# Half-array fp32 products of a two-block layer, recorded as units

## The chip, the cores and the metric

The kernel runs on one core of a Trainium2 chip. The metric is the device time of one execution in microseconds, the median of the runs. The program is one launch: it reads 159 MB of fp32 weights and constants and writes a 256 x 1024 result.

## What is computed

The input is 256 tokens of 1024 features. Two transformer-like blocks follow one another.

```
block 1: u = rmsnorm(x);  p = u @ w_in + b_in
         y_attn = sliding-window attention, 16 heads of 64, 2 key/value heads, with sinks
         y_hgrn = gated recurrence, 8 heads of 128 x 128, in chunks of 64 tokens
         x += (sigmoid(ga) * (y_attn @ wa) + sigmoid(gb) * (y_hgrn @ wh)) @ w_out
         x += (silu(u2 @ wg) * (u2 @ wu)) @ wd          (u2 = rmsnorm(x))
block 2: mod = silu(c) @ w_ada + b_ada                  (shifts, scales, gates)
         y_ssd = state-space mixer, 8 heads of 64, state 128
         y_att = chunk attention, 8 heads of 64, with a relative bias
         x += g_m * ([y_ssd, y_att] @ w_out2)
         x += g_f * conv_ffn(...)
```

Everything is fp32. The large products with weights are computed as three products of a high and a low part (`fp32r`): the weights are split on the chip as they arrive.

## The kernel before, in words

Features lie on the 128 partitions and the 256 tokens along the free dimension. A weight tile of 128 x 1024 is loaded (`raw`), rounded to `wh` on ScalarE (now and then on VectorE), and the remainder `wl` is formed on VectorE. Eight feature blocks with three matmuls each (`group`, line 292) then make one output block: these are the projections, called the gemm here. They are by far most of TensorE's instructions.

Between them stand small products in plain fp32, each of which TensorE executes as two matmul records. Several use only half of the 128 x 128 array:

- attention scores (`attn_pair`): two heads at a time; the 64 features of head 0 lie on rows 0 to 63, those of head 1 on rows 64 to 127. A head has two products, one of 256 and one of 128 columns (names `kd,aq` in block 1, `qk` in block 2). They occupy 64 rows and 128 columns of the array.
- attention values (`attn_pair`): the output of a head has 64 features, so the products occupy 128 rows and 64 columns of the array, the left half for one head, the right half for the other (names `apt,vtok` and `apt,v`), again with 256 and with 128 columns of the moving operand.
- rows of the state-space mixer (`ssd`): for each of four pairs of heads, six products of 128 rows by 64 columns with 128 moving columns (names `m_all,X` and `ce_all,prev`).
- the second half of the recurrence scores (`hgrn_pair`): for each pair of heads four products with an output of 64 partitions and 64 moving columns (names `Q_all,hD`), all on the same half, beside four products on the whole array (names `hD,hE`).

The order is not written by hand. The program is recorded as operations on symbolic tiles; `schedule` then places them with a list scheduler: for each engine it takes the operation with the lowest key among those that can start. The keys follow the running sum of recorded TensorE time, and inside a `Chain` (attention `a1` and `a2`, recurrence `h`, state space `s`) each recorded operation has a key a fixed step after the one before it: 0.401 for `a1`, 0.613 for `h`, 0.521 for `s`, 0.419 for `a2`, in microseconds. The scheduler prices an fp32 product at 1.6667 ns a column and nothing else. `mm` records one product as one operation, so the scheduler may put projections, transposes or other products between two half-array products. Each engine is given its instructions in the order so made.

Of the kernel before, what the change touches and what calls it, by code (L numbers as in the profile page):

```python
# [16 lines left out]
P = 128  # L17
# [27 lines left out]
for _n, _w in ROW:  # L45
# [2 lines left out]
NR = _o  # L48
NCST = 128 + 128 + 384 + 128

# The program is first recorded (operations on symbolic tiles), then put in an order by a list
# scheduler, and then emitted in that order.

# weights of the list scheduler (microseconds; la and altw in nanoseconds)
OPT = dict(
    split=216.82, altp1=0, altw1=250.0, o_n3=-12.83, s_n3=0.097, o_f=-0.19, s_f=0.007, lead=9.18, tp=2.16,
    la=85.0, ahead=1.87, law=0.52, altp=2.98, altw=676.0, ada=-6.56, o_h=3.27, s_h=0.613, o_a1=-4.74,
# [9 lines left out]
SET6 = "natural_log_exp_and_others"  # L67


# products of the first blocks after a norm: the last features come last  # L70
PARTS = [list(range(6)), [6, 7]]


# [68 lines left out]
class Program:  # L142
# [5 lines left out]
        self.tags = {}  # L148
        self.seqs = defaultdict(int)

    # tiles
    def tile(self, shape, dtype, tag, name, bufs=1, pool="sb"):
        t = VTile(name, list(shape), dtype, pool, tag, bufs)
        assert self.tags.setdefault((pool, tag), bufs) == bufs, (tag, bufs)
# [2 lines left out]
        ids = np.arange(int(np.prod(shape[1:])), dtype=np.int32).reshape([1] + list(shape[1:]))  # L157
        return Ref(t, (), 0, shape[0], ids)

    # operations  # L160
    def op(self, eng, dur, fn, reads, writes, table=None, key=None, nbytes=0):
        o = Op()
        o.i, o.eng, o.dur, o.fn, o.table, o.nbytes = len(self.ops), eng, dur, fn, table, nbytes
# [53 lines left out]
        return self.op("ACT", dur, fn, reads, writes, TABLE.get(func), key)  # L217

    def either(self, out, in_, scale=None, bias=None, func=AF.Copy, key=None):
        # out = scale * in + bias on ScalarE or on VectorE  # L220
        o = self.act(out, in_, func, bias=bias, scale=scale, key=key)
        nap = sum(isinstance(x, Ref) for x in (bias, scale))
        dur = out.n * (1.0417 if in_.t.psum else 0.5208) + 68 + 61 * nap

        def f():
            v = self.nc.vector
            if scale is None and bias is None:
                v.tensor_copy(out.real(), in_.real())
            elif bias is None:
                v.tensor_scalar(out=out.real(), in0=in_.real(), scalar1=_real(scale), scalar2=None, op0=ALU.mult)  # L230
            elif scale is None:
                v.tensor_scalar(out=out.real(), in0=in_.real(), scalar1=_real(bias), scalar2=None, op0=ALU.add)
            else:
                v.tensor_scalar(out=out.real(), in0=in_.real(), scalar1=_real(scale), scalar2=_real(bias), op0=ALU.mult, op1=ALU.add)

        o.alts["DVE"] = (dur, f, None)
        return o
# [49 lines left out]
    def group(self, calls, key=None):  # L287
# [7 lines left out]
        o.cnt = len(calls)  # L295
        return o

    def tr(self, out, in_, ident, key=None):
        f = lambda: self.nc.tensor.transpose(out.real(), in_.real(), ident.real())  # L299
        return self.op("PE", 107, f, [in_, ident], [out], key=key)  # L300
# [4 lines left out]
        f = lambda: self.nc.sync.dma_start(out=_real(out), in_=_real(src))  # L305
        return self.op("SP", 475, f, reads, writes, key=self.T if key is None else key, nbytes=nbytes)

    # order
    def schedule(self):
        ops = self.ops  # L310
        for o in ops:
# [25 lines left out]
        la, tp, law, altp, altw = OPT["la"], OPT["tp"], OPT["law"], OPT["altp"], OPT["altw"]  # L337
# [1 line left out]
        slot_free = {k: [0.0] * b for k, b in self.tags.items()}  # L339

        def gate(o):
            # earliest time at which the tiles of o can be had; None when a tag is used up
            g = 0.0
            need = None
            for t in o.tiles:
                if not t.live:
                    k = (t.pool, t.tag)
                    if t.bufs == 1 and t.seq != nxt[k]:
                        return None
                    need = need or defaultdict(int)  # L350
                    need[k] += 1
            if need:
                for k, n in need.items():
                    sf = slot_free[k]
                    if len(sf) < n:
                        return None
                    g = max(g, sorted(sf)[n - 1])
            return g
# [109 lines left out]
def record(pr, d):  # L468
# [29 lines left out]
    def memset(t, val):  # L498
        pr.op("POOL", 300, lambda: nc.gpsimd.memset(t.real(), val), [], [t], key=-1.0)

    # parameters and constants
    cst_t = pr.tile([P, NCST], F32, "cst", "cst_t")
    vec_t = pr.tile([P, NV], F32, "vec", "vec_t")
    row_t = pr.tile([P, NR0], F32, "row", "row_t")
# [36 lines left out]
        o, w = ROFF[name]  # L541
        return row_t[:, o:o + w]

    # building blocks
    def wload(src, n):
        T = pr.T
        raw = pr.tile([P, RAW], F32, "raw", "raw", NRAW)
# [119 lines left out]
            self.i += 1  # L667
            return self.base + self.sp * self.i

    # attention of two heads  # L670
    def attn_pair(q, krows, vcols, bias, init, sink, yh, yl):
        xs = [t2([P, 384], "ax") for _ in range(2)]
        st = pr.tile([P, 2, 8], F32, "ast", "ast", 3)
        pss = [bank() for _ in range(2)]
        rows = [slice(64 * e, 64 * e + 64) for e in range(2)]
        for e in range(2):
            mm(pss[e][:, 0:256], q[rows[e], 128:256], krows(e)[rows[e], 0:256], True, True)
        for e in range(2):
            mm(pss[e][:, 256:384], q[rows[e], 0:128], krows(e)[rows[e], 0:128], True, True)
        for e in range(2):  # L680
            x, ps, b = xs[e], pss[e], bias(e)
            for i, (lo, hi) in enumerate(((0, 256), (256, 384))):
                def f(x=x, ps=ps, lo=lo, hi=hi, b=b, i=i, e=e):
                    nc.vector.tensor_tensor_reduce(
                        out=x[:, lo:hi].real(), in0=ps[:, lo:hi].real(), in1=b[i].real(), op0=ALU.add, op1=ALU.min,
                        scale=-1.0, scalar=_real(init(e)), accum_out=st[:, e, i:i + 1].real())

                rd = [ps[:, lo:hi], b[i]] + ([init(e)] if isinstance(init(e), Ref) else [])
                vec((hi - lo) * 1.0417 + 137, f, rd, [x[:, lo:hi], st[:, e, i:i + 1]]).cnt = 2
            for i, (lo, hi) in enumerate(((0, 256), (256, 384))):  # L690
                act(x[:, lo:hi], x[:, lo:hi], AF.Exp, bias=st[:, e, i:i + 1], scale=-1.0, accum_out=st[:, e, 2 + i:3 + i])
        if sink is not None:
            tt(st[:, :, 4:6], st[:, :, 0:2], sink.to_broadcast([P, 2, 2]), ALU.add)
            act(st[:, :, 4:6], st[:, :, 4:6], AF.Exp)
            tt(st[:, :, 2:4], st[:, :, 2:4], st[:, :, 4:6], ALU.add)
        vec(94, lambda: nc.vector.reciprocal(out=st[:, :, 6:8].real(), in_=st[:, :, 2:4].real()), [st[:, :, 2:4]], [st[:, :, 6:8]])
        pts = []
        for e in range(2):
            x = xs[e]
            either(x[:, 0:256], x[:, 0:256], st[:, e, 6:7])  # L700
            either(x[:, 256:384], x[:, 256:384], st[:, e, 7:8])
            ps = bank()
            tr(ps[:, 0:128], x[:, 256:384], ident)
            tr(ps[:, 128:256], x[:, 0:128], ident)
            tr(ps[:, 256:384], x[:, 128:256], ident)
            pt = t2([P, 384], "apt")
            either(pt, ps[:, 0:384])
            pts.append(pt)
        y = bank()
        for e in range(2):  # L710
            mm(y[rows[e], 0:256], vcols(e, 0), pts[e][:, 0:256], True, False)
        for e in range(2):
            mm(y[rows[e], 128:256], vcols(e, 1), pts[e][:, 256:384], False, True)
        either(yh, y[:, :S])
        tt(yl, y[:, :S], yh.bitcast(F32), ALU.subtract)

# [1 line left out]
    h = big("h", "h")  # L718
    dma(vec_t[:, 0:8], d["vec"][:, 0:8], 8 * 512, key=-100)
    warm = bank()  # L720
# [56 lines left out]
    v_evac(2, pv)  # L777
    hl = hl_of(u)

    # gates and queries of the recurrence  # L780
    A_all = big("yhh", "A_all", shape=[P, 4, 2, S])
    K_all = big("yhl", "K_all", shape=[P, 4, 2, S])
    Q_all = big("ml", "Q_all", shape=[P, 4, 2, S])
# [37 lines left out]
    def hgrn_pair(p):  # L821
# [25 lines left out]
            f = 2 * p + j  # L847
            stt(D4[:, j, 0:192], K[:, j, 0:192], omlb[:, f:f + 1], D4[:, j, 0:192], ALU.mult, ALU.mult)
        tt(Q, B, Q, ALU.mult)
        # scores in blocks of two chunks: within the chunks, then from the second chunk to the first  # L850
        aT = aTs[p % 2]
        ps = bank([P, 2, 2, P])
        for j in range(2):
            for i in range(2):
                sl = slice(i * P, (i + 1) * P)
                mm(ps[:, j, i, :], E2[:, j, sl], Dm[:, j, sl], True, True)
                mm(ps[0:64, j, i, 64:128], D4[:, j, i * P:i * P + 64], Q[:, j, i * P + 64:i * P + 128], True, True)
        for j in range(2):
            vec(335, lambda j=j, ps=ps: nc.vector.copy_predicated(aT[:, j].real(), cmask_t.real(), ps[:, j].real()),
                [cmask_t, ps[:, j], aT[:, j]], [aT[:, j]])  # L860
# [14 lines left out]
        for j in range(2):  # L875
            mm(ps[:, j, :], KT[:, j, :], vh(j, 0), True, True)
        either(ST, ps[:, 0:2])
        # outputs by token, so that the norm of a head is a scalar of the partition
        o = bank([P, 2, 2, P])
        for j in range(2):  # L880
            mm(o[:, j, 0, :], aT[:, j, 0, :], vh(j, 0), True, True)
# [54 lines left out]
        attn1_unit(2 * p)  # L936
        attn1_unit(2 * p + 1)

    # output gate of the recurrence
    hgs = []  # L940
    for p in range(4):
        sg = t2([P, 2, S], "hg")
# [4 lines left out]
            act(sg[:, j, :], b[:, j, :], AF.Sigmoid, bias=V("b_in", T_HG + 2 * p + j))  # L947
        hgs.append(sg)

    # merge of the branches  # L950
    dma(crow, d["rows"][0:1, NR - 1024:NR].to_broadcast([P, D]), D * 512, key=pr.T - 40)
    act(crow, crow, AF.Silu)
    hA = hl_of(yA)
# [97 lines left out]
            tt(mod[:, 16:48], mod[:, 16:48], V("b_ada", 16, 32), ALU.add)  # L1051
            stt(fac[:, 1], mod[:, 32:40], 1.0, V("norm_ffn_w_2", 0, 8), ALU.add, ALU.mult)

# [1 line left out]
    w2 = d["w2"]  # L1055
    xbc = big("yhl", "xbc")
    NG = 4
# [76 lines left out]
    def ssd():  # L1134
# [68 lines left out]
                tt(m, m, cb[:, g:g + 1, :].to_broadcast([P, 4, P]), ALU.mult)  # L1203
        for f in range(4):
            y = bank()
            for i in range(2):
                for e in range(2):
                    hh = 2 * f + e
                    g, eh = divmod(hh, 4)
                    r0 = 64 * e  # L1210
                    c0 = i * P
                    hc = slice(64 * hh, 64 * hh + 64)
                    mm(y[r0:r0 + 64, c0:c0 + 128], X[i][:, hc], m_all[:, i, g, eh, :], True, i == 0)
                    if i == 1:
                        mm(y[r0:r0 + 64, c0:c0 + 128], prev[:, hc], ce_all[:, g, eh, :], False, True)
            stt(ys[:, f, :], xs[:, f, :], V("d_skip", f), y[:, :S], ALU.mult, ALU.add)

    y2 = pair("u", "y2")
# [197 lines left out]
```

## Time and profile before

| what | us |
|---|---|
| runs of the kernel | 803.27, 804.10, 804.19 (median 804.1) |
| span of the profiled execution, first to last instruction | 801.7 |
| TensorE busy in the span | 791.0 |
| VectorE busy | 604.7 |
| ScalarE busy | 497.3 |
| stretch 53 to 165: attention and recurrence of block 1 | 112 |
| stretch 519 to 584: attention and state space of block 2 | 65 |

The profile gives the span of the profiled execution; the runs, which are timed around the whole launch, lie 2.4 us above it by the median. Busy time of TensorE says little by itself, because its matmuls are pipelined and overlap: how long a product costs is read from the starts of the instructions around it.

### The profile page before, as it was taken

The page shows a single profiled execution, that of the slowest core. Times are in us where ns is not written, and L with a number is a line of the kernel's source. Part 1 is how long each engine was busy: PE and PEld are TensorE (multiplying, and loading weights), DVE is VectorE, ACT ScalarE, POOL GpSimd, SP SyncE. Part 2 cuts the span into 40 slices and gives each one's busy share as a digit, 9 for nine tenths or more (in the row PEclk, how much of TensorE's full clock was granted, in tenths as well). Part 3 has the DMA queues.
Part 4 walks back from the last instruction along what each step waited for, and adds up shares of the span by engine and source line. Part 5 has one row for each costly group of instructions (what it writes and reads, how often), then busy time and mean ns, then how long its engine had stood idle before and what let it go on. Part 6 is the DMA issues. An engine that isn't in the chain of part 4 may idle for free.

```text
span 801.7 us, 16002 instructions
## 1 busy us (share of the span) xinstructions
PE 791.0 (99%) x6362; PEld 759.5 (95%) x6362; DVE 604.7 (75%) x1104; ACT 497.3 (62%) x910; POOL 2.2 (0%) x13
## 2 busy tenths in 40 slices
PE   8999999999999999999999999999999999999996
PEld 7998999899999999999999999977799999999995
DVE  6985876778767788776768869966378988987552
ACT  6688999884445675444444559566466866556451
POOL 1000000000000000000000000000000000000000
PEclk9999999999999999999999999999999999999998
DMA  8945424459787658988778984652334666665731
GB/s 276 334 146 158 126 86 132 131 181 339 259 281 255 183 160 289 328 277 282 261 250 286 327 273 135 190 179 82 97 109 138 202 200 209 200 181 148 214 94 53
DMA packets 47803, 161.39 MB, mean 201 GB/s; under 512 B 5600, under 2 KB 8304, under 8 KB 47600
## 3 DMA queue, kind: packets, MB, share of 16 engines
q1 hardware_dynamic: 47728, 160.37, 62.6%
q8 instruction: 50, 0.82, 0.4%
q14 instruction: 25, 0.20, 0.1%
HBM read 159.03 MB, written 1.06 MB: 200 GB/s over the span
## 4 chain that ended last, share of the span: by engine, by line
PE 97%; DMA 1%; SPq 1%; DVE 0%; ACT 0%; issue 0%; DVEq 0%
PE ps L292 87%; PE ps L284 8%; PE ps L299 2%; DMA raw<-in_wv_dram 1%; SPq L305 1%; DVE ot L255 0%; DVE wl L255 0%; ACT r L215 0%; ACT wh L215 0%; DVE x L261 0%; ACT sql L215 0%; DVEq L1411 0%
## 5 line engine op out<-in xcount | busy, mean ns | idle before, releaser
L215 ACT ACTIVATE wh<-raw 128x1024 fp32r<-128x1024 f32 (+3 forms) x253 | 256.9, 1021 | 211.1 <-PE ps L292 144.1
L255 DVE TENSOR_TENSOR wl<-raw,wh 128x1024 fp32r<-128x1024 f32 (+3 forms) x257 | 300.3, 1175 | 81.8 <-ACT wh L215 78.1
L292 PE MATMUL ps<-u1h,wh 128*128 128x256 f32 x360 | 106.8, 297 | 0.0
L292 PE MATMUL ps<-u1h,wl 128*128 128x256 f32 x360 | 101.3, 281 | 0.0
L292 PE MATMUL ps<-u1l,wh 128*128 128x256 f32 x360 | 101.0, 280 | 0.0
L292 PE MATMUL ps<-uf2h,wl 128*128 128x256 f32 x320 | 90.1, 282 | 0.0
L292 PE MATMUL ps<-uf1h,wl 128*128 128x256 f32 x320 | 90.1, 282 | 0.0
L292 PE MATMUL ps<-uf2h,wh 128*128 128x256 f32 x320 | 89.8, 281 | 0.0
L292 PE MATMUL ps<-uf1h,wh 128*128 128x256 f32 x320 | 89.8, 280 | 0.0
L292 PE MATMUL ps<-uf1l,wh 128*128 128x256 f32 x320 | 89.7, 280 | 0.0
L292 PE MATMUL ps<-uf2l,wh 128*128 128x256 f32 x320 | 89.7, 280 | 0.0
L261 DVE SCALAR_TENSOR_TENSOR raw<-raw,crow 128x1024 f32<-128x1024 f32 x48 | 58.5, 1222 | 40.5 <-DMA raw<-in_wada_dram 40.4
L292 PEld LDWEIGHTS ps<-u1h,wh 128*128 128x128 f32 x360 | 68.0, 189 | 2.2 <-issue 1.5
L292 PEld LDWEIGHTS ps<-u1l,wh 128*128 128x128 f32 x360 | 67.9, 189 | 0.0
L292 PEld LDWEIGHTS ps<-u1h,wl 128*128 128x128 f32 x360 | 67.7, 188 | 0.0
L292 PEld LDWEIGHTS ps<-uf1h,wh 128*128 128x128 f32 x320 | 60.6, 189 | 0.0
L292 PEld LDWEIGHTS ps<-uf2h,wh 128*128 128x128 f32 x320 | 60.5, 189 | 0.0
L292 PEld LDWEIGHTS ps<-uf2l,wh 128*128 128x128 f32 x320 | 60.2, 188 | 0.0
L292 PEld LDWEIGHTS ps<-uf1l,wh 128*128 128x128 f32 x320 | 60.2, 188 | 0.0
L292 PEld LDWEIGHTS ps<-uf2h,wl 128*128 128x128 f32 x320 | 60.1, 188 | 0.0
L292 PEld LDWEIGHTS ps<-uf1h,wl 128*128 128x128 f32 x320 | 60.1, 188 | 0.0
L292 PE MATMUL ps<-zh,wh 128*128 128x256 f32 x176 | 49.5, 281 | 0.0
(320 smaller groups left out, 2048.0 us busy)
## 6 DMA issues: line engine op xcount, KB each, us to landing
raw<-in_wi_dram SPq DMA_DIRECT2D x49, 512.0 KB, 4.6
raw<-in_wada_dram SPq DMA_DIRECT2D x48, 512.0 KB, 4.6
raw<-in_wup_dram SPq DMA_DIRECT2D x44, 512.0 KB, 4.3
raw<-in_wd_dram SPq DMA_DIRECT2D x32, 512.0 KB, 4.3
raw<-in_wg_dram SPq DMA_DIRECT2D x22, 512.0 KB, 4.5
raw<-in_wu_dram SPq DMA_DIRECT2D x22, 512.0 KB, 5.0
raw<-in_w_dram SPq DMA_DIRECT2D x20, 512.0 KB, 4.4
raw<-in_wo_dram SPq DMA_DIRECT2D x16, 512.0 KB, 3.7
```

The lines of the kernel that those rows point to most:

```text
L215: self.nc.scalar.activation(out.real(), in_.real(), func, **kw)
L255: f = lambda: self.nc.vector.tensor_tensor(out=out.real(), in0=in0.real(), in1=in1.real(), op=op)
L261: self.nc.vector.scalar_tensor_tensor(out=out.real(), in0=in0.real(), scalar=_real(scalar), in1=in1.real(), op0=op0, op1=op1, **kw)
L284: f = lambda: self.nc.tensor.matmul(out.real(), lhsT.real(), rhs.real(), start=start, stop=stop)
L292: self.nc.tensor.matmul(out.real(), a.real(), b.real(), start=start, stop=stop)
L299: f = lambda: self.nc.tensor.transpose(out.real(), in_.real(), ident.real())
L305: f = lambda: self.nc.sync.dma_start(out=_real(out), in_=_real(src))
```

## The change

A new recording helper, `batch`, records a list of plain fp32 matmuls as one operation. The scheduler places it as a whole: the operation waits for the inputs of all its products, and nothing comes between them. Its price in the scheduler is the sum of the prices of its products. Four places use it: the four score products of a head pair, the four value products of a head pair, the six products of a pair of state-space heads, and the recurrence scores (one unit of four whole-array products, one of four half-array products). In the state-space unit the two products of a step stand next to each other, one for each half. The remaining lines of the diff drop comments. The scheduler's weights are as before, but a unit counts as one step of a `Chain`, so that the keys behind it change, and with them the places of other operations.

```
+    def batch(self, calls, key=None):
+        dur = sum(c[2].n * 1.6667 + 1 for c in calls)
+        def f():
+            for out, a, b, start, stop in calls:
+                self.nc.tensor.matmul(out.real(), a.real(), b.real(), start=start, stop=stop)
+        return self.op("PE", dur, f, [x for c in calls for x in (c[1], c[2])], [c[0] for c in calls], key=key)
...
 (attn_pair, scores)
-        for e in range(2):
-            mm(pss[e][:, 0:256], q[rows[e], 128:256], krows(e)[rows[e], 0:256], True, True)
-        for e in range(2):
-            mm(pss[e][:, 256:384], q[rows[e], 0:128], krows(e)[rows[e], 0:128], True, True)
+        pr.batch([(pss[e][:, lo:lo + n], q[rows[e], 128 - lo // 2:256 - lo // 2], krows(e)[rows[e], 0:n], True, True)
+                  for lo, n in ((0, 256), (256, 128)) for e in range(2)])
...
 (attn_pair, values)
-            mm(y[rows[e], 0:256], vcols(e, 0), pts[e][:, 0:256], True, False)
-            mm(y[rows[e], 128:256], vcols(e, 1), pts[e][:, 256:384], False, True)
+        pr.batch([(y[rows[e], 0:256], vcols(e, 0), pts[e][:, 0:256], True, False) for e in range(2)]
+                 + [(y[rows[e], 128:256], vcols(e, 1), pts[e][:, 256:384], False, True) for e in range(2)])
...
 (hgrn_pair)
-                mm(ps[:, j, i, :], E2[:, j, sl], Dm[:, j, sl], True, True)
-                mm(ps[0:64, j, i, 64:128], D4[:, j, i * P:i * P + 64], Q[:, j, i * P + 64:i * P + 128], True, True)
+        pr.batch([(ps[:, j, i, :], E2[:, j, o:o + P], Dm[:, j, o:o + P], True, True) for j, i, o in ji])
+        pr.batch([(ps[0:64, j, i, 64:128], D4[:, j, o:o + 64], Q[:, j, o + 64:o + P], True, True) for j, i, o in ji])
...
 (ssd)
-                    mm(y[r0:r0 + 64, c0:c0 + 128], X[i][:, hc], m_all[:, i, g, eh, :], True, i == 0)
-                    if i == 1:
-                        mm(y[r0:r0 + 64, c0:c0 + 128], prev[:, hc], ce_all[:, g, eh, :], False, True)
+                parts[0].append((y0, X[0][:, hc], m_all[:, 0, g, eh, :], True, True))
+                parts[1].append((y1, X[1][:, hc], m_all[:, 1, g, eh, :], True, False))
+                parts[2].append((y1, prev[:, hc], ce_all[:, g, eh, :], False, True))
+            pr.batch(sum(parts, []))
```

TensorE in block 2, the values of the first head pair, before: `apt,v` are the value products, `u2h,wh` and its neighbours the gemm.

```order
L292 MATMUL ps<-u2h,wl 128x256
L284 MATMUL ps<-apt,v_6313 64x256
L292 MATMUL ps<-u2h,wh 128x256
L292 MATMUL ps<-u2l,wh 128x256
L292 MATMUL ps<-u2h,wl 128x256
L284 MATMUL ps<-apt,v_6313 64x256
```

The same place in the changed kernel:

```order
L292 MATMUL ps<-u2h,wl 128x256
L304 MATMUL ps<-apt,v_6313 64x256 x2
L304 MATMUL ps<-apt,v_6321 64x128 x2
L292 MATMUL ps<-u2h,wh 128x256
L292 MATMUL ps<-u2l,wh 128x256
```

Before, a gemm triple stands between the products of the two heads, and the two 128-column products come later in the same way; now all four are neighbours.

TensorE in block 2, products of the state-space mixer, before:

```order
L284 MATMUL ps<-m_all,X 64x128
L292 MATMUL ps<-u2h,wh 128x256
L292 MATMUL ps<-u2l,wh 128x256
L292 MATMUL ps<-u2h,wl 128x256
L284 MATMUL ps<-m_all,X 64x128
```

The first units of them in the changed kernel:

```order
L292 MATMUL ps<-u2h,wl 128x256
L304 MATMUL ps<-m_all,X 64x128 x4
L304 MATMUL ps<-ce_all,prev 64x128 x2
L304 MATMUL ps<-m_all,X 64x128 x4
L304 MATMUL ps<-ce_all,prev 64x128 x2
L292 MATMUL ps<-u2h,wh 128x256
```

The 24 products, which were spread over the attention of the last two head pairs, now stand in four units, two of them back to back.

TensorE in block 1, the scores of the second head pair (`kd,aq`) and the recurrence scores (`hD,hE` whole array, `Q_all,hD` half), before:

```order
L284 MATMUL ps<-kd,aq 128x128 x2
L284 MATMUL ps<-Q_all,hD_736 64x64
L284 MATMUL ps<-hD,hE_731 128x128
L284 MATMUL ps<-Q_all,hD_736 64x64
L284 MATMUL ps<-hD,hE_731 128x128
L284 MATMUL ps<-Q_all,hD_736 64x64
```

And now:

```order
L304 MATMUL ps<-hD,hE_730 128x128 x4
L304 MATMUL ps<-kd,aq 128x256 x2
L304 MATMUL ps<-kd,aq 128x128 x2
L304 MATMUL ps<-Q_all,hD_728 64x64 x4
L292 MATMUL ps<-u1h,wh 128x256
```

Whole-array and half-array products alternated; now each kind stands together.

## Rows read from the trace of the kernel before

**Rows 1.** The page: shares of the chain that ended last, by line.
```profile
PE ps L292 87%; PE ps L284 8%; PE ps L299 2%; DMA raw<-in_wv_dram 1%; SPq L305 1%; DVE ot L255 0%; DVE wl L255 0%; ACT r L215 0%; ACT wh L215 0%; DVE x L261 0%; ACT sql L215 0%; DVEq L1411 0%
```

**Rows 2.** Stretches: bounds, length, then each engine's busy time; TensorE's clock, DMA.
```profile
165.00:300.00 135.00, 135.00 (x1140) 134.95 (x1140) 104.82 (x165) 76.98 (x114) 0.00 (x0) 1.00 0.74 242
53.00:165.00 112.00, 112.00 (x910) 101.70 (x909) 83.60 (x203) 100.13 (x266) 0.00 (x0) 1.00 0.42 124
...
519.00:584.00 65.00, 65.00 (x395) 47.22 (x394) 36.08 (x105) 37.63 (x92) 0.00 (x0) 1.00 0.39 122
584.00:610.00 26.00, 26.00 (x216) 25.69 (x215) 21.51 (x40) 17.46 (x31) 0.00 (x0) 1.00 0.46 143
```

**Rows 3.** Timeline of PE, block 1, four scores together: start, length, instruction.
```profile
53.51 0.28 PE L292 MATMUL ps<-u1h,wl 128*128 128x256 f32 x1
53.71 0.92 PE L284 MATMUL ps<-kd,aq 64*128 64x256 f32 x8
...
54.79 0.28 PE L292 MATMUL ps<-u1l,wh 128*128 128x256 f32 x1
```

**Rows 4.** Timeline of PE, block 2, scores alone, 256 and 128 columns.
```profile
518.96 0.28 PE L292 MATMUL ps<-u2h,wl 128*128 128x256 f32 x1
519.17 0.70 PE L284 MATMUL ps<-qk 64*128 64x256 f32 x2
...
520.02 0.28 PE L292 MATMUL ps<-u2l,wh 128*128 128x256 f32 x1
...
522.65 0.28 PE L292 MATMUL ps<-u2h,wl 128*128 128x256 f32 x1
522.86 0.48 PE L284 MATMUL ps<-qk 64*128 64x128 f32 x2
...
523.49 0.28 PE L292 MATMUL ps<-u2l,wh 128*128 128x256 f32 x1
```

**Rows 5.** Timeline of PE, block 1, four value products together.
```profile
102.50 0.28 PE L292 MATMUL ps<-u1h,wl 128*128 128x256 f32 x1
102.71 0.87 PE L284 MATMUL ps<-apt,vtok 128*64 128x256 f32 x8
...
103.74 0.28 PE L292 MATMUL ps<-u1l,wh 128*128 128x256 f32 x1
```

**Rows 6.** Timeline of PE, block 2, a value product alone, 256 columns.
```profile
534.75 0.28 PE L292 MATMUL ps<-u2h,wl 128*128 128x256 f32 x1
534.96 0.65 PE L284 MATMUL ps<-apt,v 128*64 128x256 f32 x2
...
535.76 0.28 PE L292 MATMUL ps<-u2l,wh 128*128 128x256 f32 x1
```

**Rows 7.** Timeline of PE, block 2, a state-space product alone, 128 columns.
```profile
566.51 0.28 PE L292 MATMUL ps<-u2h,wl 128*128 128x256 f32 x1
566.72 0.43 PE L284 MATMUL ps<-m_all,X 128*64 128x128 f32 x2
...
567.30 0.28 PE L292 MATMUL ps<-u2l,wh 128*128 128x256 f32 x1
```

**Rows 8.** Timeline of PE, block 1, recurrence scores in alternation.
```profile
61.08 0.49 PE L284 MATMUL ps<-hD,hE 128*128 128x128 f32 x2
...
61.75 0.49 PE L284 MATMUL ps<-hD,hE 128*128 128x128 f32 x2
```

**Rows 9.** Timeline of PE, block 2, first use of the normed state-space features.
```profile
587.50 0.28 PE L292 MATMUL ps<-y2h,wh 128*128 128x256 f32 x1
587.77 0.39 PE L292 MATMUL ps<-y2l,wh 128*128 128x256 f32 x1
```

**Rows 10.** Timeline of ACT, block 2, one exponent of attention.
```profile
522.52 0.50 ACT L215 ACTIVATE ax<-ax,ast 128x256 f32<-128x256 f32 x1
```

**Rows 11.** Waits, 500 to 615: who waited for whom, total, times, longest.
```profile
ACT wh L215 <- PE ps L292: 19.0, 14, 2.9
```

**Rows 12.** Groups of instructions: the remainder of a weight tile on VectorE.
```profile
L255 DVE TENSOR_TENSOR wl<-raw,wh 128x1024 fp32r<-128x1024 f32 (+3 forms) x257 | 300.3, 1175 | 81.8 <-ACT wh L215 78.1 <-PE ps L284 2.6
```

More of the change, by code (lines that the diff above doesn't have):

```diff
@@ L709, in attn_pair @@
         y = bank()
-        for e in range(2):
-            mm(y[rows[e], 0:256], vcols(e, 0), pts[e][:, 0:256], True, False)
-        for e in range(2):
-            mm(y[rows[e], 128:256], vcols(e, 1), pts[e][:, 256:384], False, True)
+        pr.batch([(y[rows[e], 0:256], vcols(e, 0), pts[e][:, 0:256], True, False) for e in range(2)]
+                 + [(y[rows[e], 128:256], vcols(e, 1), pts[e][:, 256:384], False, True) for e in range(2)])
         either(yh, y[:, :S])
@@ L852, in hgrn_pair @@
         ps = bank([P, 2, 2, P])
-        for j in range(2):
-            for i in range(2):
-                sl = slice(i * P, (i + 1) * P)
-                mm(ps[:, j, i, :], E2[:, j, sl], Dm[:, j, sl], True, True)
-                mm(ps[0:64, j, i, 64:128], D4[:, j, i * P:i * P + 64], Q[:, j, i * P + 64:i * P + 128], True, True)
+        ji = [(j, i, i * P) for j in range(2) for i in range(2)]
+        pr.batch([(ps[:, j, i, :], E2[:, j, o:o + P], Dm[:, j, o:o + P], True, True) for j, i, o in ji])
+        pr.batch([(ps[0:64, j, i, 64:128], D4[:, j, o:o + 64], Q[:, j, o + 64:o + P], True, True) for j, i, o in ji])
         for j in range(2):
@@ L1205, in ssd @@
             y = bank()
[L1206 to L1212, printed above, removed]
-                    mm(y[r0:r0 + 64, c0:c0 + 128], X[i][:, hc], m_all[:, i, g, eh, :], True, i == 0)
-                    if i == 1:
-                        mm(y[r0:r0 + 64, c0:c0 + 128], prev[:, hc], ce_all[:, g, eh, :], False, True)
+            parts = [[], [], []]
+            for e in range(2):
+                hh = 2 * f + e
+                g, eh = divmod(hh, 4)
+                hc = slice(64 * hh, 64 * hh + 64)
+                y0, y1 = (y[64 * e:64 * e + 64, c:c + P] for c in (0, P))
+                parts[0].append((y0, X[0][:, hc], m_all[:, 0, g, eh, :], True, True))
+                parts[1].append((y1, X[1][:, hc], m_all[:, 1, g, eh, :], True, False))
+                parts[2].append((y1, prev[:, hc], ce_all[:, g, eh, :], False, True))
+            pr.batch(sum(parts, []))
             stt(ys[:, f, :], xs[:, f, :], V("d_skip", f), y[:, :S], ALU.mult, ALU.add)
```

## The prediction

> **What bounds the kernel now.** I read the page's chain first, then busy time by stretch, then TensorE's timeline around single small products, then the waits. TensorE is busy 791 of 801.7 us, and of the chain that ended last 87% lie on the gemm line 292 and 8% on line 284, where all small fp32 products stand [rows 1]. Nothing else waits long on the path, so whatever shortens TensorE's sequence shortens the time, as long as the others keep up. The steady gemm gives the unit of measure: 1140 records in 135.00 us, 0.1184 us each, all at the full clock (granted 1.00) [rows 2].
>
> A small product costs more than its own stream, and the reader can take the cost from starts alone: the start of the second gemm record behind it, minus the start of the last gemm record before it, minus two gemm steps (0.237). Four score products together: 54.79 - 53.51 - 0.237 = 1.043 us [rows 3]. One score product alone: 0.823 with 256 columns and 0.603 with 128 [rows 4]. So 128 columns stream for 0.22 us, and going to the half-row arrangement and back costs 0.603 - 0.22 = 0.383. Two such pairs of products, each pair side by side, make 0.383 + 0.44 + 0.22 = 1.043, exactly what the four cost together; one after the other they would be 1.70. So the two heads run at the same time when they are neighbours, and one changeover serves all four.
>
> The same for outputs on half the columns: four value products together cost 103.74 - 102.50 - 0.237 = 1.003 [rows 5], one alone with 256 columns 0.773 [rows 6], one with 128 columns, a state-space product, 0.553 [rows 7]. Stream 0.22 per 128 columns again, changeover 0.333, and 0.333 + 0.66 = 0.993 for the four side by side.
>
> **The change part by part.** I counted in the two orders of TensorE how often it changes arrangement, and how many half-array products have no partner.
>
> Scores, block 2. Before, 16 products, each in a run of its own: 8 x 0.823 + 8 x 0.603 = 11.41 us. Now four units of four at 1.043: 4.17. Saved: 7.2 us.
>
> Values and state-space rows, block 2. Before, 16 + 24 products in 32 runs. Changeovers 32 x 0.333 = 10.66; streams 8 x 0.44 + 8 x 0.22 + 24 x 0.22 = 10.56, less four products that happen to lie beside one of the other half (0.88); together 20.34. Now eight units in seven runs: 7 x 0.333 = 2.33, streams 8 x 0.66 = 5.28; together 7.61. Saved: 12.7 us.
>
> Block 1. The scores already stand in fours and gain nothing. The recurrence scores alternate: one round of a whole and a half product takes 61.75 - 61.08 = 0.67 us [rows 8], which is 0.22 + 0.11 (64 columns) + 0.333 = 0.66. All in all, half a changeover at each change (0.19 to or from half rows, 0.167 for half columns, 0.18 taken between the two, an estimate from these): before 11, 45 and 5 changes, 10.5 us; now 15, 23 and 1, 6.9 us. Saved 3.6 us. Besides, before, in four head pairs the 256-column value products and in three the 128-column ones are parted, and then stream one after the other: 4 x 0.44 + 3 x 0.22 = 2.4 us. Saved together: 6.0 us.
>
> Sum on TensorE: 7.2 + 12.7 + 6.0 = 26 us.
>
> Unseen in the trace are the six state-space products as a unit. They come as three neighbours of different halves; side by side a unit is 0.333 + 0.66 = 0.99, one after the other 0.333 + 1.32 = 1.65, which is 4 x 0.66 = 2.6 us more in all. I take the first: the value products, with the same halves and the same arrangement, do it in [rows 5]. The Trainium skill, "TensorE: Matmul & The Clock Gate", Part 3, "The mechanism", says that a weight load overlaps with a running matmul only when the two are on different row groups; products on half the columns use all row groups, so by that sentence the six would go one after the other, and the sum would be 23.4 instead of 26. The trace disagrees with it for the values: 1.003 us for four, where one after the other would be 1.65.
>
> What it adds: waits. A unit waits for the last of its inputs, and behind it on TensorE stands the gemm, on which everything else depends. One place can be read. The statistics of the state-space output are followed by gemm triples on the attention features, and only then come the normed features; before, nine triples cover that chain, and the first matmul that needs the new features starts 0.27 us behind the one before it, where a step is 0.12 [rows 9], so there is no slack. In the new order one of the nine stands ahead of the statistics instead: cover less by 3 x 0.118, a wait longer by 0.36 us.
>
> The others have no price in this trace, since TensorE ran behind everybody in this stretch: ScalarE alone waited 19.0 us for it to release weight buffers [rows 11]. That lead goes with the 20 us. The bounds: nothing, if the chains still come in time; or one exponent (0.50 us, the longest step of the attention chain [rows 10]) before each of the 12 units of block 2, 6 us. The nearest rows are [rows 9], where the one chain without a lead costs TensorE 0.15; 12 of these are 1.8. I take 2.
>
> As to the other engines: from 519 to 584 VectorE is busy 36.1 of 65 us and ScalarE 37.6 [rows 2]. With 20 us gone, 45 are left, ScalarE's share rises to 0.84 and VectorE's to 0.80, and their instructions overlap at the ends in the timeline, so the real load is below that. Converting weights is still hidden, and the transfers use 0.39 of the DMA engines there. In block 1 ScalarE is the fuller one: 100.1 of 112 us [rows 2], which becomes 0.94 of 106. With 266 instructions whose ends overlap the next by a little it is not yet the bound, and copies that either engine can do may go to VectorE, busy 83.6; I charge nothing there, and the upper end of the range is for it too.
>
> Balance: 26 - 0.36 - 2 = 23.6 us; the span 801.7 becomes 778.1. The runs' median lies 2.4 above the span, and launch and tail are not touched: 780.5 us.
>
> **The rivals.**
>
> (a) Column halves do not run side by side in the state-space units: 2.6 us more, 783.1. For it speaks the sentence cited; against it [rows 5].
>
> (b) ScalarE and VectorE become the bound in block 2. At the share that ScalarE reaches in the next stretch, 17.46 / 26 = 0.67 [rows 2], its 37.6 us need 56 us instead of 45: 11 us come back, 791.5. For it: order changes on all engines, and the attention chain passes through both several times per head pair. Against it: no row shows TensorE waiting there, and VectorE has room to take conversions. The Trainium skill says as much in "TensorEngine Tiling (Array Packing)", "PSUM Bottleneck": tiling speeds up TensorE but not the evacuation, which may become the bottleneck; no row here shows that yet, and by it the time would go toward this rival.
>
> (c) Slower: head of line. If VectorE puts a weight's remainder (1.175 us [rows 12]) ahead of the last input of a unit, the unit and the gemm behind it stand for that long. There are 24 units in block 1 (8 scores, 8 values, 8 recurrence) and 12 in block 2; if all were hit, 36 x 1.175 = 42 us, 818. It decides from 23 units on (26 / 1.175 = 22). Against it: block 1's scores already stand together and TensorE waits for none of them.
>
> (d) The units are emitted but the changeover is paid by each product anyway, inside a unit: then only the streams side by side are gained. Against it: [rows 3, 5], where it is paid once. About 800, no gain to speak of.
>
> **How the numbers follow.** The forecast's own case (776 to 783): 0.62. Rival (a), or waits of some 2 to 6 us more than taken, 783 to 788: 0.20. Rival (b): 0.09. Rival (c): 0.03; (d): 0.02. Below 776, with no new waits at all and cheaper changes in block 1: 0.04. The range 776 to 788 holds the first two cases, 0.82. This measurement can tell about 0.2% from no change, 1.6 us. Faster by more: 0.96; within: 0.01; slower: 0.03.
>
> **What would show it.** In the profile after: a unit of scores in block 2 costs about 1.04 by the starts around it, a unit of values 1.0, a state-space unit 0.99 (1.65 by (a)); the alternation in block 1 is gone. Line 304 holds the half-array products. The stretch from the first score product of block 2 to the statistics shrinks from 65 to about 47 us, that from 53 to 165 by 6, and all stretches without these products keep their length. Wrong would be: TensorE with idle time of more than about 4 us between 510 and 565, waiting for exponents, transposed copies or weights (b or c); or a step of the gemm other than 0.118.

## The result, and the profile after

The changed kernel takes 779.8 us (median of four runs, 779.7 to 781.7) against 803.7 for the kernel before on the same chip. The ratio is 0.971, 95% interval 0.9697 to 0.9723. The forecast was 780.5 with a range of 776 to 788. The span of the profiled execution is 778.0, the forecast's 778.1.

The chain that ended last, by line, in the changed kernel (it answers to [rows 1]); line 304 is the new helper:

```profile
PE ps L292 88%; PE ps L304 3%; PE ps L284 2%; PE ps L309 2%; DMA raw<-in_wv_dram 1%; DMA abc<-adr 1%; SPq L315 1%; ACT ax L215 1%; ACT wh L215 0%; DVE ot L255 0%; DVE wl L255 0%; ACT m_all L215 0%; ACT qk L215 0%; DVE m_all L261 0%; ACT ce_all L215 0%
```

The small products went from 8% of 802 us (line 284) to 5% of 778 (lines 304 and 284). A line of ScalarE, the exponents of attention (`ACT ax`), now stands on the chain with 1%; before, no line of ScalarE or VectorE had more than 0%: in places the lead that they had is used up.

Busy time by stretch in the changed kernel (bounds, length, then TensorE, weight loads, VectorE, ScalarE, POOL, clock, DMA), which answers to [rows 2]: attention and recurrence of block 1; block 2 from the first scores to the statistics; the gemm stretch behind block 1's attention.

```profile
53.00:159.00 106.00, 106.00 (x907) 99.18 (x906) 82.62 (x205) 99.90 (x266) 0.00 (x0) 1.00 0.40 126
513.00:560.30 47.30, 45.96 (x396) 41.30 (x395) 34.58 (x103) 36.64 (x94) 0.00 (x0) 1.00 0.49 155
159.00:294.00 135.00, 135.00 (x1141) 134.95 (x1140) 104.11 (x164) 75.18 (x110) 0.00 (x0) 1.00 0.74 246
```

Almost the same number of TensorE records, 907 against 910, takes 106 us instead of 112; in block 2, 396 against 395 take 47.3 instead of 65. The bounds of these stretches are round numbers, good to about half a microsecond. The plain gemm is untouched: 1141 records in 135.00 us, as before. ScalarE is busy 0.94 of the first stretch and 0.77 of the second, and the first shows no TensorE idle time at all.

The units themselves, in the timeline of TensorE of the changed kernel (start, length, instruction): scores, values and state-space rows of block 2, each with the gemm record before and the second one behind.

```profile
513.04 0.28 PE L292 MATMUL ps<-u2h,wl 128*128 128x256 f32 x1
513.25 0.92 PE L304 MATMUL ps<-qk 64*128 64x256 f32 x8
...
514.33 0.28 PE L292 MATMUL ps<-u2l,wh 128*128 128x256 f32 x1
...
524.62 0.28 PE L292 MATMUL ps<-u2h,wl 128*128 128x256 f32 x1
524.83 0.87 PE L304 MATMUL ps<-apt,v 128*64 128x256 f32 x8
...
525.85 0.28 PE L292 MATMUL ps<-u2l,wh 128*128 128x256 f32 x1
...
537.08 0.28 PE L292 MATMUL ps<-u2h,wl 128*128 128x256 f32 x1
537.29 0.66 PE L304 MATMUL ps<-m_all,X 128*64 128x128 f32 x8
...
538.97 0.28 PE L292 MATMUL ps<-u2l,wh 128*128 128x256 f32 x1
...
542.97 0.28 PE L292 MATMUL ps<-u2h,wl 128*128 128x256 f32 x1
543.18 0.66 PE L304 MATMUL ps<-m_all,X 128*64 128x128 f32 x8
...
544.22 0.28 PE L292 MATMUL ps<-u2l,wh 128*128 128x256 f32 x1
```

With two gemm steps (0.237) taken off as in the prediction: scores 1.05 (forecast 1.04), values 0.99 (1.0), one state-space unit 1.01 (0.99). The two units that stand back to back from 537.29 on cost 538.97 - 537.08 - 0.237 = 1.65, which is one changeover of 0.333 and six pairs of 0.22. Before, a score product alone cost 0.60 to 0.82 [rows 4], and a half-column one 0.55 to 0.77 [rows 6, 7].

The waits that came in their place stand before transposes in block 2 (the bracket is the idle time and its releaser):

```profile
529.86 0.28 PE L292 MATMUL ps<-u2h,wl 128*128 128x256 f32 x1
530.81 0.55 PE L309 MATMUL ps<-cst_t,ax 128*128 128x128 f32 x3 [0.67 <-ACT ax L215]
...
539.47 0.28 PE L292 MATMUL ps<-u2h,wl 128*128 128x256 f32 x1
540.41 0.55 PE L309 MATMUL ps<-cst_t,ax 128*128 128x128 f32 x3 [0.67 <-ACT ax L215]
```

Twice the transpose starts 0.95 us behind the gemm record where a step is 0.12, 1.7 us in all, since an exponent or the scaling behind it comes late on ScalarE. (The bracket counts from the modelled end of the record before, hence 0.67.) ScalarE in turn waits far less for TensorE to free weight buffers; this row answers to [rows 11], from 500 to 592 in the changed kernel:

```profile
ACT wh L215 <- PE ps L292: 7.5, 8, 1.8
```

### The profile page after: what moved, and what is told of

Its sections match the earlier page's. It is cut to its first block, busy times and chain, and to the rows that moved or that the text cites. A ratio compares the mean times of both kernels' runs of the same rounds, so it can differ in the third digit from the quotient of the medians.

```text
span 778.0 us, 15993 instructions
## 1 busy us (share of the span) xinstructions
PE 766.2 (98%) x6362; PEld 751.2 (97%) x6362; DVE 603.4 (78%) x1104; ACT 495.9 (64%) x910; POOL 2.2 (0%) x13
## 4 chain that ended last, share of the span: by engine, by line
PE 94%; DMA 2%; ACT 2%; DVE 1%; SPq 1%; issue 0%; DVEq 0%
PE ps L292 88%; PE ps L304 3%; PE ps L284 2%; PE ps L309 2%; DMA raw<-in_wv_dram 1%; DMA abc<-adr 1%; SPq L315 1%; ACT ax L215 1%; ACT wh L215 0%; DVE ot L255 0%; DVE wl L255 0%; ACT m_all L215 0%; ACT qk L215 0%; DVE m_all L261 0%; ACT ce_all L215 0%
```

## The experiments

My theory was that of the prediction: a run of half-array products costs one changeover (0.383 for half rows, 0.333 for half columns), and products on different halves run side by side. The rivals: only one of these two counts, or the gain is an accident of the new order on the other engines.

**The order inside a unit (e1_halves).**

```
-                  for lo, n in ((0, 256), (256, 128)) for e in range(2)])
+                  for e in range(2) for lo, n in ((0, 256), (256, 128))])
...
 (the same for the values)
...
-            pr.batch(sum(parts, []))
+            pr.batch([p[e] for e in range(2) for p in parts])
```

> All units as in the changed kernel, in the same order, but inside a unit of scores, values or state-space rows the products of one half stand first and then those of the other (256, 128, 256, 128 instead of 256, 256, 128, 128; three and three instead of three pairs). Changeovers are as many as in the changed kernel. My theory (one changeover a run, and neighbours of different halves run side by side): the 28 units lose the pairs; each costs 0.66 us more if nothing overlaps at the seam between the halves (28 x 0.66 = 18.5 us, 798), 0.44 more if the last product of one half still runs beside the first of the other (12.3 us, 792). Rival: only the number of changeovers counts, the order inside a unit does not: 780, as the changed kernel.

Measured: 781.4 us (780.2 to 782.0), ratio 0.9718 (0.9702 to 0.9734), nowhere near 792 or 798. My numbers missed and the rival's came. Either pairing is worth nothing, or it does not need neighbours. The timeline of TensorE in this kernel shows the latter; a score unit of block 1, then a state-space unit and a value unit of block 2:

```profile
52.66 0.28 PE L292 MATMUL ps<-u1h,wl 128*128 128x256 f32 x1
52.87 0.93 PE L304 MATMUL ps<-kd,aq 64*128 64x256 f32 x8
...
53.95 0.28 PE L292 MATMUL ps<-u1l,wh 128*128 128x256 f32 x1
...
544.82 0.29 PE L292 MATMUL ps<-u2h,wl 128*128 128x256 f32 x1
545.03 0.71 PE L304 MATMUL ps<-m_all,X 128*64 128x128 f32 x6
...
546.33 0.28 PE L292 MATMUL ps<-u2l,wh 128*128 128x256 f32 x1
...
548.62 0.28 PE L292 MATMUL ps<-u2h,wl 128*128 128x256 f32 x1
548.83 0.88 PE L304 MATMUL ps<-apt,v 128*64 128x256 f32 x8
...
549.86 0.28 PE L292 MATMUL ps<-u2l,wh 128*128 128x256 f32 x1
```

The score unit still costs 53.95 - 52.66 - 0.237 = 1.05, so the halves ran side by side although two products of one half are recorded ahead of the other half's. The value unit, on column halves, also keeps its price with two ahead of two: 549.86 - 548.62 - 0.237 = 1.00. With three ahead of three, the state-space unit costs 1.27 instead of 1.01: part of the pairing is lost, 0.26 of the 0.66. The single records of the trace agree: with two ahead, the other half starts 0.015 us behind the first, with three ahead 0.275. So being neighbours is not the condition. Two products of one half ahead cost nothing, three did; that this unit uses column halves does not explain it, since the value unit lost nothing. Whether the number alone decides was not tested. What running side by side is worth needed another experiment.

**All products on one half (e5_onehalf).**

```
-        pr.batch([(pss[e][:, lo:lo + n], q[rows[e], 128 - lo // 2:256 - lo // 2], krows(e)[rows[e], 0:n], True, True)
+        pr.batch([(pss[e][:, lo:lo + n], q[rows[0], 128 - lo // 2:256 - lo // 2], krows(0)[rows[0], 0:n], True, True)
```

> The changed kernel, but both heads of a score unit use the rows of head 0 (queries and keys), so that all four products stand on the same half of the rows; the scores of head 1 are thus not computed, head 0's take their place. Order, number of instructions and changeovers are those of the changed kernel. The products of the two halves ran side by side in the first experiment even where they were not neighbours, so the order inside a unit does not show what running side by side is worth; this does. My theory: products of one half run one after the other, a score unit costs 0.383 + 4 x 0.44 x 0.75 = 1.70 us instead of 1.04, 12 units: 7.9 us more than the changed kernel, 787.8. Rival (the gain is changeovers alone; two products of one half overlap as well): 780.

Measured: 786.8 us (786.4 to 787.8), ratio 0.9793 (0.9777 to 0.981), 7.0 above the changed kernel; 7.9 was expected. The score unit in this kernel's timeline:

```profile
53.54 0.28 PE L292 MATMUL ps<-u1h,wl 128*128 128x256 f32 x1
53.74 1.57 PE L304 MATMUL ps<-kd,aq 64*128 64x256 f32 x8
...
55.47 0.28 PE L292 MATMUL ps<-u1l,wh 128*128 128x256 f32 x1
```

55.47 - 53.54 - 0.237 = 1.69 (expected 1.70) instead of 1.05. Same instructions, same order, same changeover: the difference is that the two heads no longer use different rows. 12 units by 0.64 are 7.7; most of the rest was given back where the changed kernel waits for exponents (0.4 us of such idle time in this kernel instead of 1.3). The rival falls: running side by side is worth 0.64 us a unit of scores.

**A changeover inside a unit (e6_parted) and its control (e7_tail).**

```
 (e6_parted)
+        pr.batch(sc[:2] + [(pss[0][:, 384:512], ones["1"], ones["1"], True, True)] + sc[2:])
+            pr.batch(sp[:2] + [(y[:, 256:384], ones["1"], ones["1"], True, True)] + sp[2:])
 (e7_tail)
+        pr.batch(sc[:4] + [(pss[0][:, 384:512], ones["1"], ones["1"], True, True)] + sc[4:])
+            pr.batch(sp[:6] + [(y[:, 256:384], ones["1"], ones["1"], True, True)] + sp[6:])
```

Here `sc` is the list of the four products of a score unit and `sp` that of the six of a state-space unit.

> The changed kernel with one more product in each of the 12 score units and the 4 state-space units: ones times ones on the whole array, 128 columns, into columns of the bank that nobody reads; it stands behind the first two products, so that TensorE leaves the half arrangement and comes back inside the unit. To be compared with e7_tail, whose order is the same except that the extra product stands at the unit's end. My theory: 11 score units pay 0.383 more than there, one that is followed by half-column products 0.2, and the state-space units, which stand two by two, pay two changeovers of 0.333 more in all: 5.1 us above e7_tail, about 789. Rival (a changeover costs nothing in itself): the same as e7_tail.

> As e6_parted, the extra product at the end of each unit. My theory: 16 x 0.22 us of stream and 0.3 to 0.7 for units that no longer stand back to back come to the changed kernel's 780: 784. The scheduler moves other work a little, 1 us either way.

Measured: e6_parted 788.7 (788.2 to 789.5), e7_tail 785.7 (784.3 to 787.3). The difference is 3.1 us where 5.1 was expected; e7_tail came out 1.7 above its number. The runs of e7_tail spread over 3 us, so a unit's price is better read from the timelines, e6_parted first, then e7_tail:

```profile
53.14 0.28 PE L292 MATMUL ps<-u1h,wl 128*128 128x256 f32 x1
53.35 0.70 PE L304 MATMUL ps<-kd,aq 64*128 64x256 f32 x4
53.98 0.49 PE L304 MATMUL ps<-ones 128*128 128x128 f32 x2
54.40 0.49 PE L304 MATMUL ps<-kd,aq 64*128 64x128 f32 x4
...
55.04 0.28 PE L292 MATMUL ps<-u1l,wh 128*128 128x256 f32 x1
```

```profile
53.14 0.28 PE L292 MATMUL ps<-u1h,wl 128*128 128x256 f32 x1
53.34 0.92 PE L304 MATMUL ps<-kd,aq 64*128 64x256 f32 x8
54.20 0.49 PE L304 MATMUL ps<-ones 128*128 128x128 f32 x2
...
54.65 0.28 PE L292 MATMUL ps<-u1l,wh 128*128 128x256 f32 x1
```

The same five products cost 1.66 with the whole-array one in the middle and 1.27 with it at the end: 0.39 for leaving the half rows and coming back, 0.383 by [rows 4]. For half columns, two state-space units stand together (first product, then the first gemm record behind them; e6_parted, then e7_tail):

```profile
547.10 0.44 PE L304 MATMUL ps<-m_all,X 128*64 128x128 f32 x4
...
549.70 0.38 PE L292 MATMUL ps<-u2h,wh 128*128 128x256 f32 x1
```

```profile
543.83 0.66 PE L304 MATMUL ps<-m_all,X 128*64 128x128 f32 x8
...
546.10 0.36 PE L292 MATMUL ps<-u2h,wh 128*128 128x256 f32 x1
```

Both hold the same products; e6_parted has three runs of half-column products there, e7_tail two. 2.60 against 2.27 us: 0.33 for the one run more, 0.333 by [rows 7]. Both changeovers thus stand with their prices. Over all units, the profiled executions differ by 4.1 us (spans 787.7 and 783.6). Block 1 gives what was expected: up to the last gemm record before the first scores of block 2 the difference is 518.38 - 515.49 = 2.9, and 7 x 0.383 + 0.2 is 2.9. Block 2 gives 1.2 instead of 2.2; there e7_tail waits more than e6_parted, for exponents (0.4 us of idle time) and inside a value unit (its price is 1.33 instead of 1.00), so a part of the longer sequence is covered by waits.

**Each place alone (e2_att, e3_ssd, e4_rec).** Only the named `batch` calls are left in, the other places record one by one as before.

> Only the attention units (scores and values); recurrence scores and state-space rows are recorded one by one as before. My theory: block 2's scores save 7.2 us, the C runs there go from 32 to 23 (3.0 us) and the values pair up (about 2.2 net), block 1's parted values pair up (2.4) with some 0.7 of changeovers: 15.5, less about 1 of new waits: 14.5 us faster than before, 789.5. Rival (the gain is an accident of the new order on the other engines, not of changeovers and pairs): no relation to these numbers.

> Only the state-space rows are units; all else one by one as before. My theory: half-column runs in block 2 go from 32 to 18, 14 x 0.333 = 4.7 us, and 24 products stream as 12 pairs, 2.6 less the 0.9 that chance pairs gave before: 6.4 us on TensorE; new waits of 0 to 4 us come off: 798 to 801. Rival (six products do not run side by side): 1.7 less, 800 to 803.

> Only the recurrence scores are units; all else one by one as before. My theory: nine fewer half-column runs in block 1 at 0.333 would be 3.0 us, part of it eaten since runs that used to lie next to each other no longer do: 1.8 to 3 us faster, 801 to 802.3. Rival (the alternation cost nothing): 804.

| kernel | us, median | ratio to before (interval) | span | against 801.7 |
|---|---|---|---|---|
| attention alone | 791.0 | 0.9839 (0.9824 to 0.9853) | 788.3 | -13.4 |
| state-space rows alone | 798.9 | 0.9937 (0.9922 to 0.9952) | 797.3 | -4.4 |
| recurrence scores alone | 802.7 | 0.9995 (0.998 to 1.0009) | 800.4 | -1.3 |
| all (changed kernel) | 779.8 | 0.971 (0.9697 to 0.9723) | 778.0 | -23.7 |

The spans are of one execution each, and runs of one kernel differ by 1 to 2 us. Attention came 1.5 us above its number, which speaks against the rival that the gain is an accident of the new order; the state-space rows came inside their range, which overlaps that of their rival; what decides between the two is the unit's price, 1.01 in the changed kernel. The recurrence missed: its runs cannot be told from no change. Its span is 1.3 shorter, and its timeline shows a place where a part of the rest went:

```profile
64.69 0.65 PE L284 MATMUL ps<-apt,vtok 128*64 128x256 f32 x2
...
67.01 0.86 PE L284 MATMUL ps<-apt,vtok 128*64 128x256 f32 x6
```

The value products, still recorded one by one, are parted: one runs alone at 64.69, three at 67.01. By the order of the records, the 256-column value products are parted in seven of the eight head pairs of this kernel; before, they were in four, and the 128-column ones in three. By the prices of the prediction that streams 0.7 us more (7 x 0.44 against 2.4). A gain in one place is spent when the scheduler fills other single products in. So the parts do not add: the spans fall by 19.1 alone, by 23.7 together. Counted in the orders, half-column runs in block 2 fall by 9 and by 14 alone and by 25 together, in block 1 by 2 and 9 alone and by 13 together: four runs or 1.3 us. The parted values are 0.7, and the state-space kernel waits 1.7 us for weight remainders, 0.6 before. The other 1.5 us of the difference, about what the spans scatter, I have not assigned.

**A further step (e8_mode, e9_weights).** If each run costs a changeover, the scheduler should know the arrangement.

```
+                    if e == "PE" and o.mode != pmode:
+                        s += OPT["mq"] if pmode else 0.0
...
+            if e == "PE":
+                pmode = o.mode
```

> A version that should beat both. Units as in the changed kernel; besides, the scheduler knows in which arrangement (whole array, half rows, half columns) the product placed last on TensorE stands, and once it has left the whole array it prefers the products of the arrangement it is in; the weights of the chains were chosen anew with that. By the order, runs on half columns fall from 12 to 8 in block 1 and from 7 to 4 in block 2, and the tail transposes wait no longer for exponents. My theory (each run costs its changeover): 7 x 0.333 = 2.3 us, and the waits of the changed kernel in block 2, some 1.7 us, go: 776. Rival (what is left of changeovers is covered by waits anyway): 780.

> As e8_mode with the same weights but without the preference, so that the order has 12 and 8 runs on half columns, as the changed kernel (12 and 7). My theory: what e8_mode gains is mostly the preference: about 780 to 782 here. Rival (the new weights do it): 776 as e8_mode.

Measured: e8_mode 778.8 (778.2 to 779.6), ratio 0.9694 (0.9677 to 0.971); e9_weights 784.2, ratio 0.9757 (0.9742 to 0.9772). With these weights the preference is worth 5.4 us, but against the changed kernel, which has other weights, only 1.0 us is left, and the intervals of the ratios overlap: no clear win, and 2.8 short of the forecast. TensorE's waits for exponents are gone from e8_mode, as expected, but it now waits 0.8 us behind the statistics for the normed features (ACT y2h 0.5, DVE y2l 0.3), where the changed kernel has no such wait. e9_weights missed its 780 to 782: its eight runs more than e8_mode are 2.7 us by their price, and it waits 1.7 us for weight remainders instead of 0.6. So changeovers can still be bought off; how much of what remains the chains of the other engines would let through, these two kernels do not show.

## Why the prediction was right

**What a product costs.** Right, with its sizes: changeovers of 0.383 and 0.333 and streams of 0.22 per 128 columns, read from single products, gave the cost of units within 0.02 us, that of the state-space unit too, which no row of before showed (1.01 for 0.99, and 1.65 for two). But the prediction said that the two heads run at the same time "when they are neighbours". That condition fell with e1_halves: two of one half ahead of the other half's change nothing, three cost 0.26. In the kernel before, other arrangements stood between the products of the two heads.

**The sum on TensorE.** A little too high, and the span's 778.0 for 778.1 is in part luck. The first score product of block 1 in the changed kernel:

```profile
53.33 0.92 PE L304 MATMUL ps<-kd,aq 64*128 64x256 f32 x8
```

From it to the first of block 2 (513.25) it is 459.92 us, before 519.17 - 53.71 = 465.46 [rows 3, 4]: block 1 gained 5.5, put at 6.0. From there to the end of the span it is 264.75, before 282.53: block 2 gained 17.8, put at 7.2 + 12.7 less 2.4 of waits, 17.5. The missing 0.4 of the 23.7 lies ahead of the first unit and is chance: that product starts anywhere from 52.9 to 53.7 in the kernels here. With the waits that came (below), TensorE's sequence shrank by about 25, not 26. By the prices that e5, e6 and e7 confirm, the 26 split into changeovers, 12 x 0.383 + 25 x 0.333 + 3.6 = 16.5 us, and products running side by side, 26 - 16.5 = 9.5.

**From the span to the runs.** The forecast put the runs 2.4 us above the span, the median of three runs against the span of one execution. In the changed kernel they lie 1.8 above it (779.8 and 778.0), and so do single runs of every kernel here above their own spans. This makes most of the 0.7 us between 780.5 and 779.8.

**The sentence of the Trainium skill** ("TensorE: Matmul & The Clock Gate", Part 3, "The mechanism"), by which weight loads overlap with running matmuls only when the row group differs: it speaks of weight loads, and that the products of a state-space unit would then go one after the other was my inference. The traces decide against that for these column halves, 1.01 us a unit where 1.65 would be needed. Rival (a) is out.

**The waits.** The 2 us taken for the other chains came as 1.7, before the transposes, not before the units as the bound had it. That the size fits is luck too: it was 12 times a wait at another place. The one wait that I priced from rows, 0.36 us longer at the normed state-space features, did not come:

```profile
563.97 0.28 PE L292 MATMUL ps<-y2h,wh 128*128 128x256 f32 x1
564.09 0.35 PE L292 MATMUL ps<-y2l,wh 128*128 128x256 f32 x1
564.27 0.28 PE L292 MATMUL ps<-y2h,wl 128*128 128x256 f32 x1
```

These rows of the changed kernel answer to [rows 9], where the step from `y2h,wh` to `y2l,wh` was 0.27; now it is 0.12, a plain step, and the one behind it 0.18, 0.06 more than a step. The step that failed: I held the chain from statistics to features constant. First TensorE's statistics product and ScalarE in the changed kernel, then the same before:

```profile
560.68 0.59 PE L284 MATMUL ps<-sql,ones_s 128*128 128x256 f32 x2
...
559.75 0.37 ACT L215 ACTIVATE y2h<-ps 128x256 fp32r<-128x256 f32 x1
560.13 1.28 ACT L474 ACT_TABLE_LOAD   x1
561.42 0.47 ACT L215 ACTIVATE r<-ps,eps 128x256 f32<-128x256 f32 x1
```

```profile
583.88 0.59 PE L284 MATMUL ps<-sql,ones_s 128*128 128x256 f32 x2
...
583.46 0.38 ACT L215 ACTIVATE y2h<-ps 128x256 fp32r<-128x256 f32 x1 [1.56 <-PE ps L284]
583.86 1.28 ACT L464 ACT_TABLE_LOAD   x1
585.15 0.47 ACT L215 ACTIVATE r<-ps,eps 128x256 f32<-128x256 f32 x1
```

The table load stands behind the copy of the last value product, and the statistics' logarithm (`r<-ps,eps`) behind the load. Before, that copy waited 1.56 us for the last value product, which ran just ahead of the statistics. Now the values come as a unit well ahead of them (558.64), the table is in place earlier, and the logarithm starts 0.74 us behind the start of the statistics product instead of 1.27: the chain is 0.5 us shorter, more than the 0.36 of cover that it lost.

**The rivals.** (b) fell: the stretch took 47.3 us, not 56, with ScalarE at 0.77 in it, above the 0.67 on which the rival stood. (c) fell: in the changed kernel not one unit on line 304 shows up among TensorE's waits. Its 818 is a span; as a run it would have been 820. (d) fell with the units themselves, 1.05 for four scores, and with e6_parted, where a second changeover shows its price. Its "about 800" was also mis-sized: by its own terms the streams side by side would remain, the 9.5 us above, and the time would be about 795.

## What to carry to other kernels

On TensorE count the changes between whole-array and half-array products in program order, not only the products: here each round trip cost 0.33 to 0.39 us, more than the 0.22 us that a product of 128 columns streams. Products on opposite halves belong in the same run, alternating or two and two, since that makes one of two free; with three ahead of three a part was lost. If a scheduler sets the order, give it such products as one unit, all kinds at once: with units in the recurrence alone, it scattered the value products more than before.

## What the runs showed of the hardware that was not expected

fp32 products of different halves run side by side without being neighbours: with two products of one half recorded ahead, a score unit cost 1.05 us against 1.05 in alternation; with three ahead, a state-space unit cost 1.27 against 1.01; with all on one half, a score unit cost 1.69.
